# Two edits to a decoder trunk: where the feed-forward's down steps stand, and a written order for layer A's first projections

## The chip, the cores and the metric

The kernel runs on one core of one Trainium2 chip. The metric is the time of one execution on the device, in microseconds; less is better. Several engines of the core work side by side and wait for each other by semaphores: TensorE (PE) multiplies matrices and transposes, with its weight loads shown as an engine of their own (PEld); VectorE (DVE) and ScalarE (ACT) work element by element and are the ones here that read PE's results from its banks; GpSimd (POOL) works element by element on on-chip memory; SyncE (SP) issues most transfers, and POOL issues some.

## The reference, cut to what matters

A two-layer decoder trunk over 1024 tokens of width 1024, in float32. Layer A has sparse attention, layer B dilated attention over shared keys and values; each layer ends with a gated feed-forward of hidden width 2816.

```python
h = rmsnorm(x, norm_mix[layer])
proj = h @ w_in                      # layer A: queries, three kinds of keys and values, gates
k_cmp = compress(kvh(kc), pe_k, w1_k, w2_k)
...
x = x + mix
a, b = jnp.split(rmsnorm(x, norm_ffn[layer]) @ w_up, 2, axis=-1)
x = x + (jax.nn.silu(a) * b) @ w_down
```

In layer A a table of position biases (32 buckets by 16 heads) is added to all attention scores.

## The kernel before, in words

**Precision.** Every float32 operand of a large product is split in two parts, high and low: ACT copies it to the high part (lines 348 and 351, or `ph` at line 1002) and DVE subtracts that from the operand to get the low part (lines 349 and 352, `pl` at line 1003). A product is then three matmuls (`mm3`, lines 375 to 377): high by high, high by low and low by high.

**Layer A's first stage.** It runs in three rounds over row blocks of 128 tokens: blocks 0 and 1, then 2 and 3, then 4 to 7. `norm_to_hT` normalises each block (ACT squares and sums at line 382, takes the root at 384; DVE takes the reciprocal at 385 and scales at 395), PE turns it (line 400), and ACT and DVE split the result into `hH` and `hL`. After each round `proj_T` projects the tokens that are ready to the keys that will be compressed (two weight blocks of 128 columns), and ACT and DVE copy the result to `kc2` (lines 577 to 581). After the last round come the bias table's products (`bias_rows`, lines 451 to 463, with the one-hot table loaded in four pieces), then the projection of all eight row blocks to the window values and gates (`tok_proj` with `evac_v(1)`, 304 columns), then the compression, which reads `kc2`, and the remaining projections. A small table, `blockind`, is split and stored in two halves through one buffer (lines 703 to 710). In this part nothing but the framework's planner sets the order of instructions on each engine: it lists them by program order and by when it reckons their operands to be ready, and what it has placed runs in that order.

**The feed-forward.** Hidden blocks j = 0 to 21 of 128 columns are taken in pairs. Each j has seven up steps (`cols_steps`), one Strassen-like product of four k-blocks by three matmuls each, 12 matmuls; in the trace they go by the block that they multiply: m1 B11, m2 B21, m5 T1, m6 T2, m7 T3, m4 T4, m3 B22. m1, m6, m7 and m4 add up in one bank (`ux`), with an ACT copy taken out after each of the first three (`d0` at line 1218, `d1` at 1257, `c` at 1266); m2 goes to bank `uy`, is added to `d0` by DVE (line 1227), and m5 and m3 then add up in `uy`. `d0` and `d1` are built in the pair's own blocks `u[base + 0]` and `u[base + 1]`. They go through Silu (line 1415) and are multiplied by the other half (line 1417). The four blocks `u` of a pair are taken in turn from six, so that the last two of a pair are the first two of the pair before.

Each pair also has seven down steps (`down_steps`, `rows_steps`), in the order D0 to D6, that multiply its four hidden blocks with the down weights, again 12 matmuls each. D0, D3, D4 and D6 write the banks `dx`, one after another; D1, D2 and D5 write `dr`. DVE adds the results to `xr` (line 1061). D2 and D3 first form sums of the hidden blocks and of the weights on POOL (lines 1069 to 1079). D0 issues the pair's four weight loads and, in layer 0 for some pairs, two copies of bias rows.

The up steps of a pair and the down steps of the pair before are put into one list, and `staged` prepares each step before it runs the one ahead of it. The place of the down steps in that list is this:

```python
for i, f in enumerate(steps, j == 2):
    seq.append(f)
    if i % 2 and prev:
        seq.append(prev.pop(0))
```

With the up steps of a pair counted 0 to 13, a down step follows the steps 1, 3, 5, 7, 9, 11 and 13. Here too the planner then orders each engine. Layer B's projections use the same `cols_steps`; both attentions are ordered by a planner written in the kernel (`Order`), which ends by adding an edge between each instruction and the next of its engine.

Of the kernel before, what the change touches and what calls it, by code (L numbers as in the profile page):

```python
# [11 lines left out]
F32 = mybir.dt.float32  # L12
F32R = mybir.dt.float32r
# [8 lines left out]
D = 1024  # L22
# [3 lines left out]
G = 4  # L26
# [88 lines left out]
class Order:  # L115
# [88 lines left out]
    def done(self):  # L204
# [75 lines left out]
        queued = mybir.DependencyInfo(mybir.DependencyClass.NoSync, mybir.DependencyReason.DATA)  # L280
        for e, row in order.items():
            if e == "SP":
                continue
            for a, b in zip(row, row[1:]):
                self.tc.add_manual_dep(b, a.name, queued, reason="order")
# [14 lines left out]
def trunk(ctx, tc, I, out):  # L300
# [28 lines left out]
    pool(ctx, "shift", "right").tile([128, 104], F32, name="shift")  # L329
# [4 lines left out]
    nc.vector.memset(eps, 1e-6)  # L334

# [18 lines left out]
    class Weights:  # L354
# [6 lines left out]
        def load(self, src, a, n, gains=None):  # L361
            raw, wh, wl = (r.tile() for r in self.rings)
            v = lambda t: t[:, :a * n].rearrange("p (a n) -> p a n", n=n)
            self.last = nc.sync.dma_start(v(raw), src.rearrange("(a p) n -> p a n", p=128))
            if gains is not None:
                nc.gpsimd.tensor_mul(v(raw), v(raw), gains.unsqueeze(2).to_broadcast([128, a, n]))
            split(wh[:, :a * n], wl[:, :a * n], raw[:, :a * n])
            return v(wh), v(wl)
# [19 lines left out]
    def norm_to_hT(p, xget, gains, hH, hL, t0, n):  # L388

        xs = []  # L390
        for t in range(t0, t0 + n):
            xt = xget(t)
            xn = p.tile([128, D], F32, name="nxn", bufs=4)
            rs = row_scale(p, xt, xn)
            nc.vector.tensor_scalar(xn, xt, rs, None, op0=OP.mult)
            xs.append(xn)
        for k in range(KC):
            pt = bank("mm")
            for i in range(n):
                nc.tensor.transpose(pt[:, i * 128:(i + 1) * 128], xs[i][:, k * 128:(k + 1) * 128], ident)  # L400
            tk = slice(t0 * 128, (t0 + n) * 128)
            split(hH[k][:, tk], hL[k][:, tk], pt[:, :n * 128], gains[:, k:k + 1])
# [15 lines left out]
    def tok_proj(ws, n, hT, tokens, evac):  # L418

        hH, hL = hT  # L420
        for t in range(NT):
# [29 lines left out]
    def bias_rows(p):  # L451
        rb = p.tile([33, H], F32, name="rb")
        nc.vector.memset(rb, 1.0)
        nc.gpsimd.dma_start(rb[0:32], I["rel_bias"])
        R = p.tile([H, NL], F32, name="R")
        for lo in range(0, NL, 512):
            n = min(512, NL - lo)
            oh = p.tile([33, 512], F32, name="oh", bufs=2)
            nc.gpsimd.dma_start(oh[:, :n], I["onehot"][:, lo:lo + n])
            ps = bank("mm")  # L460
            nc.tensor.matmul(ps[:H, :n], rb, oh[:, :n], start=True, stop=True)
            nc.vector.tensor_copy(R[:, lo:lo + n], ps[:H, :n])
        nc.gpsimd.dma_start(sR, R)
# [103 lines left out]
    with ExitStack() as c:  # L567
        wts = Weights([(pool(c, "pw", "right"), (3, 5, 5))])
        cctx = ExitStack()
# [22 lines left out]

        with ExitStack() as c2:
# [8 lines left out]
            kc2, ws = None, []  # L602
            for t0, n in ((0, 2), (2, 2), (4, 4)):
                norm_to_hT(np_, xget, g_mix[0], *hT, t0, n)
                if t0 < 4:
                    ws.append(blocks_weights(0, len(ws)))
                if t0 == 0:
                    kc2 = blocks_tile()
                done = t0 * 128, (t0 + n) * 128
                if t0 == 2:  # L610
                    proj_T(ws[0], hT, evac_c(kc2, 0), (done,))
                    proj_T(ws[1], hT, evac_c(kc2, 1), ((0, 512),))
                else:
                    for ch in range(len(ws)):
                        proj_T(ws[ch], hT, evac_c(kc2, ch), (done,))
        cp = pool(cctx, "pc")
        st = pool(c, "pst", "right")
# [50 lines left out]
        def evac_v(i):  # L668
            def f(t, ps):
                vt = st.tile([128, G, 128], F32R, name="vt", bufs=2)  # L670
                split(vt[:, :, 0:64], vt[:, :, 64:128], ps[:, :256].rearrange("p (g d) -> p g d", d=64))
                nc.gpsimd.dma_start(vS[i, t], f32(vt))
                if i == 1:
                    nc.vector.tensor_copy(gates[:, t, :], ps[:, 256:304])
            return f

        bias_rows(cp)
        tok_proj(wide(wts, W[:, 2304:2608], 304, 3), 304, hT, natural, evac_v(1))
# [24 lines left out]
        def store_blockind():  # L703
            for a in range(2):
                cols = slice(a * 512, (a + 1) * 512)
                raw = st.tile([16, 512], F32, name="bif", bufs=1)
                nc.gpsimd.dma_start(raw, I["blockind"][:, cols])
                t = st.tile([128, 512], F32R, name="sth", bufs=2)
                nc.scalar.copy(t[:16], raw)
                nc.gpsimd.dma_start(bS[:, cols], f32(t[:16]))  # L710

# [1258 lines left out]
```

## Time and profile before

| what | value |
|---|---|
| median of three runs | 2914.61 us (2912.68 to 2917.57) |
| profiled execution, its own time | 2911.7 us |
| its span, first to last instruction | 2909.9 us |
| mean granted TensorE clock | 0.990 |
| first transpose of layer A on PE | 8.33 us |
| first matmul of the compression | 88.03 us |
| PE busy, 0 to 88 us | 70.27 us |
| PE busy, 900 to 1400 us (feed-forward of layer A) | 498.44 us, 2169 matmuls |
| PE busy, 2340 to 2840 us (feed-forward of layer B) | 498.52 us, 2167 matmuls |

The profile lists busy time by engine. A matmul's record is longer than the distance between the starts of two matmuls, because they overlap on PE; rates are therefore read from starts and counts, not from durations. A window's row gives its length, the busy time and number of instructions of PE, PEld, DVE, ACT and POOL, the granted clock as a share, the busy share of the transfer engines and GB/s. In rows of waits the numbers are the total in us, how often, and the longest. In rows of the timeline they are the start and the duration in us.

### The profile page before, as it was taken

The page shows a single profiled execution, that of the slowest core. Times are in us where ns is not written, and L with a number is a line of the kernel's source. Part 1 is how long each engine was busy: PE and PEld are TensorE (multiplying, and loading weights), DVE is VectorE, ACT ScalarE, POOL GpSimd, SP SyncE. Part 2 cuts the span into 40 slices and gives each one's busy share as a digit, 9 for nine tenths or more (in the row PEclk, how much of TensorE's full clock was granted, in tenths as well). Part 3 has the DMA queues.
Part 4 walks back from the last instruction along what each step waited for, and adds up shares of the span by engine and source line. Part 5 has one row for each costly group of instructions (what it writes and reads, how often), then busy time and mean ns, then how long its engine had stood idle before and what let it go on. Part 6 is the DMA issues. An engine that isn't in the chain of part 4 may idle for free.

```text
span 2909.9 us, 43844 instructions
## 1 busy us (share of the span) xinstructions
PE 2817.3 (97%) x14766; PEld 2376.1 (82%) x14766; DVE 2255.6 (78%) x4465; ACT 1520.9 (52%) x3314; POOL 1540.8 (53%) x1776
## 2 busy tenths in 40 slices
PE   7999999999999999999999999899999999999997
PEld 6988899998877888888787888788877788888885
DVE  5441999997488888988876777598965888888887
ACT  5431888886443333333554444689855433333334
POOL 2134877873165555555546786455522655555551
PEclk8999999999999999999999999999999999999999
DMA  5756243212122322231225555966521221111112
GB/s 161 237 156 190 67 111 89 59 26 117 30 69 66 83 62 66 62 83 52 95 80 146 161 167 160 281 194 184 142 88 37 73 61 51 55 55 58 51 44 76
DMA packets 266833, 294.46 MB, mean 101 GB/s; under 512 B 18099, under 2 KB 209475, under 8 KB 266608
## 3 DMA queue, kind: packets, MB, share of 16 engines
q1 hardware_dynamic: 246960, 231.50, 27.5%
q0 software_dynamic: 19648, 60.16, 6.9%
q8 instruction: 117, 1.92, 0.3%
q14 instruction: 108, 0.88, 0.1%
HBM read 228.49 MB, written 78.81 MB: 106 GB/s over the span
## 4 chain that ended last, share of the span: by engine, by line
PE 72%; DVE 16%; ACT 4%; issue 3%; DMA 2%; POOL 2%; SPq 1%; DVEq 0%; ACTq 0%; POOLq 0%
PE ux L375 5%; PE ux L376 5%; PE ux L377 5%; DVE pl L1003 5%; PE pt L485 5%; DVE xr L1061 4%; PE uy L375 4%; PE uy L376 4%; PE uy L377 4%; PE dx L376 4%; PE dx L377 4%; PE dx L375 3%; PE dr L375 3%; PE mm L375 3%; PE mm L376 3%
## 5 line engine op out<-in xcount | busy, mean ns | idle before, releaser
L1003 DVE TENSOR_TENSOR pl<-oT,ph 128x512 fp32r<-128x512 f32 x325 | 323.6, 1016 | 73.2 <-ACT ph L1002 64.1
L1002 ACT ACTIVATE ph<-oT 128x512 fp32r<-128x512 f32 x325 | 196.4, 626 | 221.8 <-PE ux L376 60.2
L485 PE MATMUL pt<-ident,P 128*128 128x128 f32 x1536 | 260.3, 277 | 4.8 <-DVE tl L349 2.3
L1003 DVE TENSOR_TENSOR pl<-oTb,ph 128x512 fp32r<-128x512 f32 x235 | 218.2, 954 | 50.6 <-ACT ph L1002 42.3
L1002 ACT ACTIVATE ph<-oTb 128x512 fp32r<-128x512 f32 x235 | 140.4, 625 | 177.3 <-PE ux L376 52.5
L1061 DVE TENSOR_TENSOR xr<-xr,dr 128x512 f32<-128x512 f32 x320 | 204.6, 679 | 29.2 <-PE dr L377 29.2
L1386 POOL TENSOR_TENSOR oT<-oT,gffn 128x512 f32<-128x512 f32 x92 | 106.7, 1168 | 205.5 <-DMA oT<-in_ffn_w_up_dram 168.5
L349 DVE TENSOR_TENSOR tl<-pt,th 128x512 fp32r<-128x512 f32 (+1 forms) x320 | 194.2, 625 | 20.9 <-ACT th L348 17.3
L485 PEld LDWEIGHTS pt<-ident,P 128*128 128x128 f32 x1536 | 181.5, 141 | 28.3 <-POOL P L924 4.1
L924 POOL TENSOR_SCALAR P<-P,sm,gates 128x384 f32<-128x384 f32 (+7 forms) x256 | 182.6, 723 | 38.6 <-DVE sm L922 32.6
L1061 DVE TENSOR_TENSOR xr<-xr,dx 128x512 f32<-128x512 f32 x320 | 200.1, 680 | 2.4 <-PE dx L377 1.8
L348 ACT ACTIVATE th<-pt 128x512 fp32r<-128x512 f32 (+1 forms) x320 | 168.4, 545 | 42.9 <-PE pt L485 33.0
L1386 POOL TENSOR_TENSOR oTb<-oTb,gffn 128x512 f32<-128x512 f32 x92 | 103.8, 1138 | 154.5 <-DMA oTb<-in_ffn_w_up_dram 134.7
L920 ACT ACTIVATE P<-P,m 128x384 f32<-128x384 f32 (+7 forms) x256 | 171.1, 671 | 12.4 <-DVE m L918 9.0
L1761 ACT ACTIVATE P<-P,st 128x384 f32<-128x384 f32 (+2 forms) x256 | 139.4, 548 | 6.2 <-DVE st L1756 5.2
L376 PE MATMUL dx<-pl,ph 128*128 128x512 f32 x352 | 139.3, 396 | 1.0
L377 PE MATMUL dx<-ph,pl 128*128 128x512 f32 x352 | 136.5, 391 | 0.0
L510 PE MATMUL o<-tl,V 128*128 128x256 f32 x476 | 136.3, 304 | 0.0
L509 PE MATMUL o<-th,V 128*128 128x256 f32 x476 | 135.9, 300 | 0.2 <-DVE oTb L522 0.2
L1756 DVE CUSTOM_DVE_ANT_0 P<-s,T 128x384 f32<-128x384 f32 (+2 forms) x256 | 115.7, 478 | 15.9 <-PE s L1812 5.2
L1002 ACT ACTIVATE ph<-wd 128x512 fp32r<-128x512 f32 x86 | 53.7, 629 | 115.5 <-PE ux L376 55.0
L914 DVE CUSTOM_DVE_ANT_0 P<-s,T 128x256 f32<-128x256 f32 (+3 forms) x192 | 101.8, 551 | 6.4 <-PE s L912 4.6
(951 smaller groups left out, 9530.9 us busy)
## 6 DMA issues: line engine op xcount, KB each, us to landing
qB<-xr POOLq DMA_DIRECT2D x96, 256.0 KB, 5.1
oT<-in_ffn_w_up_dram SPq DMA_DIRECT2D x92, 256.0 KB, 3.1
oTb<-in_ffn_w_up_dram SPq DMA_DIRECT2D x92, 256.0 KB, 3.0
Q<-qB SPq DMA_DIRECT2D x40, 512.0 KB, 7.8
wd<-in_ffn_w_down_dram SPq DMA_DIRECT2D x66, 256.0 KB, 2.5
oT<-in_b_w_q_dram SPq DMA_DIRECT2D x48, 256.0 KB, 4.0
K<-kBs SPq DMA_DIRECT2D x40, 256.0 KB, 9.6
wraw<-in_a_w_in_dram SPq DMA_DIRECT2D x18, 512.0 KB, 4.7
```

Source lines behind the costliest of these rows:

```text
L348: nc.scalar.activation(H_, src, AF.Copy)
L349: nc.vector.tensor_sub(L_, src, f32(H_))
L375: nc.tensor.matmul(ps, lh, rh, start=first, stop=False, skip_group_check=bool(shared))
L376: nc.tensor.matmul(ps, lh, rl, start=False, stop=False, skip_group_check=bool(shared))
L377: return nc.tensor.matmul(ps, ll, rh, start=False, stop=last, skip_group_check=bool(shared))
L485: nc.tensor.transpose(ps[:, i * 128:(i + 1) * 128], b, ident)
L920: nc.scalar.activation(P[:, e, :n], P[:, e, :n], AF.Exp, bias=mm[:, e:e + 1], scale=-1.0, accum_out=sm[:, e:e + 1])
L924: nc.gpsimd.tensor_scalar(P[:, e, :n], P[:, e, :n], sm[:, e:e + 1], gt(g, t, br, 2 * hp + e, 1), op0=OP.mult, op1=OP.mult)
L1002: nc.scalar.activation(like(h), src, AF.Copy)
L1003: (eng or nc.vector).tensor_sub(like(l), src, f32(like(h)))
L1061: nc.vector.tensor_add(xs, xs, banks[t])
L1386: nc.gpsimd.tensor_mul(v, v, gains[:, k:k + 4].unsqueeze(2).to_broadcast([128, 4, 128]))
```

## The change

In the feed-forward, the down steps follow the up steps 2, 3, 5, 8, 10, 11 and 13 of a pair, and the first product's copy `d0` of odd j from 5 on goes into the block `c` instead of the pair's own block:

```diff
             def tmp(n):
+                if n == "d0" and j > 4 and j % 2:
+                    return misc["c"]
                 if n in ("d0", "d1"):
                     return u[base + int(n[1])]
...
             for i, f in enumerate(steps, j == 2):
                 seq.append(f)
-                if i % 2 and prev:
+                if i in (2, 3, 5, 8, 10, 11, 13) and prev:
                     seq.append(prev.pop(0))
```

In layer A's first stage, normalising, turning and splitting become separate functions; the value projection of single row blocks is put between the others; the bias products and the block indicator are drawn into the stage; and the instructions of PE, ACT and DVE, up to the last turn, get the written order as an edge from each to the next (`in_turn`, cut out of `Order`). The first weight block is loaded and split in two parts, the second and third part of the value weights are loaded into row buffers, the one-hot table is loaded at once, and a square root of one column is taken at the start.

```diff
-    pool(ctx, "shift", "right").tile([128, 104], F32, name="shift")
+    shift = pool(ctx, "shift", "right").tile([128, 104], F32, name="shift")
...
+    nc.scalar.activation(shift[:, 0:1], eps, AF.Sqrt)
...
+def in_turn(tc, rows):
+    queued = mybir.DependencyInfo(mybir.DependencyClass.NoSync, mybir.DependencyReason.DATA)
+    for row in rows:
+        for a, b in zip(row, row[1:]):
+            tc.add_manual_dep(b, a.name, queued, reason="order")
...
+        def load(self, src, a, n, gains=None, parts=None, other=None):
+            raw, wh, wl = [other() if other and r is self.rings[0] else r.tile() for r in self.rings]
...
+            for c in cuts:
+                self.last = nc.sync.dma_start(v(raw)[:, c], rows[:, c])
...
+            if parts:
+                return (v(wh), v(wl)), [lambda c=c: fill(c) for c in cuts]
...
+    def turn_rows(xs, gains, hH, hL, t0, ks):
+
+        pts = [bank("mm") for _ in ks]
+        for i, xn in enumerate(xs):
+            for k, pt in zip(ks, pts):
+                nc.tensor.transpose(pt[:, i * 128:(i + 1) * 128], xn[:, k * 128:(k + 1) * 128], ident)
+        tk = slice(t0 * 128, (t0 + len(xs)) * 128)
+        return [lambda k=k, pt=pt: split(hH[k][:, tk], hL[k][:, tk], pt[:, :len(xs) * 128], gains[:, k:k + 1])
+                for k, pt in zip(ks, pts)]
...
+            start = len(nc.cur_bb.bb.instructions)
+            bias = bias_rows(np_)
+            xs = [xget(t) for t in range(2)]
+            cols = lambda ch: W[:, 1024 + 128 * ch:1152 + 128 * ch]
+            ws = [wts.load(cols(ch), KC, 128, None, 2 - ch) for ch in range(2)]
+            wv = [wts.load(W[k * 128:min(k + 3, KC) * 128, 2304:2608], min(3, KC - k), 304, None, 1,
+                           k and (lambda: np_.tile([128, D], F32, name="nx", bufs=4))) for k in (0, 3, 6)]
+            xs += [xget(t) for t in range(2, 8)]
+            fills = [f for _, fs in ws + wv for f in fs]
...
+            xn = [normed(np_, xs[t]) for t in range(2)]
+            fs = turned(xn, 0, 0, 4)
+            run(fills[:1] + fs + fills[1:2])
+            run(turned(xn, 0, 4, 8))
+            run(fills[2:3])
+            blocks(0, 2, 0)
+            run(fills[3:])
+            blocks(0, 2, 1)
+            xn = [normed(np_, xs[t]) for t in (2, 3)]
+            values(0)
+            late = []
+            values(1, late)
+            for ks in ((0, 4), (4, 8)):
+                run(turned(xn, 2, *ks) + late)
+                late = []
+            xn = [normed(np_, xs[t]) for t in (4, 5)]
+            blocks(2, 2, 0)
+            xn += [normed(np_, xs[t]) for t in (6, 7)]
+            blocks(2, 2, 1)
+            store_blockind()
+            values(2)
+            run(turned(xn, 4, 0, 4))
+            values(3)
+            bias()
+            run(turned(xn, 4, 4, 8))
...
+            in_turn(tc, [rows[e] for e in ("PE", "Activation", "DVE")])
+            blocks(4, 4, 0, 1)
+            for t in range(4, 8):
+                values(t)
```

Here `blocks(t0, n, ch)` projects n row blocks from t0 on with weight block ch to the keys to be compressed, `values(t)` projects row block t to the window values and gates, and `bias()` makes the bias table's products. SP and POOL get no written order.

More of the change, by code (lines that the diff above doesn't have):

```diff
@@ L386, in row_scale, with normed @@
         return rs
[L388 to L402, printed above, removed]
+    def normed(p, xt):
+        xn = p.tile([128, D], F32, name="nxn", bufs=4)
+        rs = row_scale(p, xt, xn)
+        nc.vector.tensor_scalar(xn, xt, rs, None, op0=OP.mult)
+        return xn
+    def turn_rows(xs, gains, hH, hL, t0, ks):
[6 more added lines that the diff above has]
+                for k, pt in zip(ks, pts)]
     def alloc_hT(p):
@@ L416, in proj_T, with tok_proj @@
             evac(ps, tk)
-    def tok_proj(ws, n, hT, tokens, evac):
+    def tok_proj(ws, n, hT, tokens, evac, ts=range(NT)):
         hH, hL = hT
-        for t in range(NT):
+        for t in ts:
             ps = bank("mm")
@@ L452, in bias_rows, with products @@
         rb = p.tile([33, H], F32, name="rb")
-        nc.vector.memset(rb, 1.0)
+        nc.gpsimd.memset(rb[32:33], 1.0)
         nc.gpsimd.dma_start(rb[0:32], I["rel_bias"])
         R = p.tile([H, NL], F32, name="R")
[L456 to L463, printed above, removed]
+        oh = p.tile([33, NL], F32, name="oh")
+        nc.gpsimd.dma_start(oh, I["onehot"])
+        def products():
+            for lo in range(0, NL, 512):
+                n = min(512, NL - lo)
+                ps = bank("mm")[:H, :n]
+                nc.tensor.matmul(ps, rb, oh[:, lo:lo + n], start=True, stop=True)
+                nc.vector.tensor_copy(R[:, lo:lo + n], ps)
+            nc.gpsimd.dma_start(sR, R)
+        return products
     def bias_skewed(t, lo, n, pitch, h, prev):
@@ L591, in blocks_weights, with evac_v, f, store_blockind @@
             return wts.load(W[:, c0:c0 + 128], KC, 128)
+        def evac_v(i):
+            def f(t, ps):
+                vt = st.tile([128, G, 128], F32R, name="vt", bufs=2)
+                split(vt[:, :, 0:64], vt[:, :, 64:128], ps[:, :256].rearrange("p (g d) -> p g d", d=64))
+                nc.gpsimd.dma_start(vS[i, t], f32(vt))
+                if i == 1:
+                    nc.vector.tensor_copy(gates[:, t, :], ps[:, 256:304])
+            return f
+        def store_blockind():
+            for a in range(2):
+                cols = slice(a * 512, (a + 1) * 512)
+                raw = st.tile([16, 512], F32, name="bif", bufs=1)
+                nc.gpsimd.dma_start(raw, I["blockind"][:, cols])
+                t = st.tile([128, 512], F32R, name="sth", bufs=2)
+                nc.scalar.copy(t[:16], raw)
+                nc.gpsimd.dma_start(bS[:, cols], f32(t[:16]))
         with ExitStack() as c2:
@@ new lines, in trunk, with run, blocks, values @@
+            ws = [w for w, _ in ws]
+            wv = [(wh[:, i], wl[:, i]) for (wh, wl), _ in wv for i in range(wh.shape[1])]
+            kc2 = blocks_tile()
+            turned = lambda xn, t0, *ks: turn_rows(xn, g_mix[0], *hT, t0, range(*ks))
+            def run(fs):
+                for f in fs:
+                    f()
+            def blocks(t0, n, *chs):
+                for ch in chs:
+                    proj_T(ws[ch], hT, evac_c(kc2, ch), ((t0 * 128, (t0 + n) * 128),))
+            def values(t, late=None):
+                ev = evac_v(1)
+                tok_proj(wv, 304, hT, natural, ev if late is None else lambda *a: late.append(lambda: ev(*a)), (t,))
@@ new lines, in trunk @@
+            xn = [normed(np_, xs[t]) for t in (4, 5)]
[8 more added lines that the diff above has]
+            run(turned(xn, 4, 4, 8))
+            rows = {}
+            for i in nc.cur_bb.bb.instructions[start:]:
+                if not type(i).__name__.startswith("Bass"):
+                    rows.setdefault(str(i.engine).split(".")[-1], []).append(i)
@@ L701, in evac_k @@
             return f
[L703 to L710, printed above, removed]
         def evac_q(ch):
```

42 lines of the change are left out of this document (6 added, 36 removed).

## The prediction

> **What bounds the kernel now.** I read the page first, then the stages as windows, then the waits of the stages that the change touches.
>
> ```profile
> span 2909.9 us, 43844 instructions
> PE 2817.3 (97%) x14766; PEld 2376.1 (82%) x14766; DVE 2255.6 (78%) x4465; ACT 1520.9 (52%) x3314; POOL 1540.8 (53%) x1776
> ```
> ```profile
> 0.00:88.00 88.00, 70.27 (x384) 59.61 (x385) 41.08 (x81) 41.81 (x81) 20.78 (x35) 0.90 0.57 162
> 88.00:290.00 202.00, 202.00 (x1092) 175.47 (x1090) 71.44 (x99) 69.67 (x105) 57.73 (x116) 1.00 0.69 197
> 900.00:1400.00 500.00, 498.44 (x2169) 405.14 (x2168) 438.64 (x597) 188.86 (x326) 280.22 (x207) 1.00 0.24 65
> 2340.00:2840.00 500.00, 498.52 (x2167) 404.87 (x2166) 434.27 (x597) 188.61 (x326) 273.01 (x205) 1.00 0.17 52
> ```
>
> PE bounds nearly everything, so only time in which PE does nothing, or works slowly, can be won. The columns are PE, PEld, DVE, ACT, POOL, then granted clock, DMA share and GB/s. From 88 to 290 us PE is busy all the time: whatever the first stage gives back there reaches the end. The two feed-forward windows look full, and DVE is busy 88% in them, so it is the next bound.
>
> **The first 88 us.** These rows give PE's waits there, then events on PE and ACT, then two stretches.
>
> ```profile
> PE mm L400 <- DVE nxn L395: 9.6, 2, 8.3
> PE mm L400 <- DVE hL L352: 6.0, 2, 3.1
> PE mm L461 <- DMA oh<-in_onehot_dram: 1.8, 1, 1.8
> ```
> ```profile
> 5.70 1.28 ACT L384 ACT_TABLE_LOAD   x1
> 6.99 0.29 ACT L384 ACTIVATE nrs<-nss,eps 128x1 f32<-128x1 f32 x1
> 12.31 1.06 ACT L382 ACTIVATE nxn<-nx 128x1024 f32<-128x1024 f32 x1 [2.42 <-DMA nx<-in_x_dram]
> 13.36 2.28 ACT L351 ACTIVATE hH<-mm,gmix 128x256 fp32r<-128x256 f32 x6
> 21.50 0.60 ACT L709 CAST sth<-bif 16x512 fp32r<-16x512 f32 x1
> 27.35 0.62 ACT L709 CAST sth<-bif 16x512 fp32r<-16x512 f32 x1
> ```
> ```profile
> 22.89 1.01 POOL L707 DMA_DIRECT2D bif<-in_blockind_dram  x1
> ```
> ```profile
> 8.33 2.91 PE L400 MATMUL mm<-ident,nxn 128*128 128x128 f32 x12 [8.33 <-DVE nxn L395]
> 15.17 0.58 PE L375 MATMUL mm<-hH,wh 128*128 128x256 f32 x1
> 37.73 4.32 PE L400 MATMUL mm<-ident,nxn 128*128 128x128 f32 x32
> 53.21 1.89 PE L461 MATMUL mm<-oh,rb 33*16 33x512 f32 x4
> 59.92 0.62 PE L375 MATMUL mm<-wh,hH 128*128 128x304 f32 x1
> 88.03 0.28 PE L375 MATMUL cmp<-bh,wh 128*128 128x256 f32 x1
> ```
> ```profile
> 24.00:32.00 8.00, 6.37 (x26) 5.57 (x27) 7.34 (x17) 6.63 (x16) 0.48 (x1) 0.57 0.63 211
> 56.00:64.00 8.00, 7.14 (x25) 4.51 (x26) 5.36 (x9) 1.97 (x3) 0.51 (x1) 0.59 0.38 93
> ```
>
> PE waits 8.3 us for the first normalised rows, then twice about 3 us for split activations. ACT shows why: the planner put the square of the third row block ahead of the splits of the first two, and that square stood 2.42 us for its load. Behind such waits PE runs slowly: 0.57 and 0.59 of the clock. The stage ends when PE starts the compression at 88.03.
>
> **The feed-forward windows.** PE's weight loads name who is late; the rows behind them are from one odd step.
>
> ```profile
> PEld ux L375 <- ACT oT L1266: 4.0, 8, 0.5
> PEld dx L376 <- DVE pl L1003: 3.9, 8, 0.5
> PEld ux L375 <- ACT ph L1002: 2.3, 6, 0.4
> PEld dx L375 <- DVE xr L1061: 1.1, 4, 0.3
> ```
> ```profile
> 1046.98 0.39 PE L375 MATMUL ux<-B11h,ph 128*128 128x512 f32 x1
> 1049.70 0.39 PE L375 MATMUL dr<-ph 128*128 128x512 f32 x1
> 1056.27 0.39 PE L377 MATMUL uy<-B21h,pl 128*128 128x512 f32 x1
> 1056.54 1.01 PE L375 MATMUL dx<-ph 128*128 128x512 f32 x2
> 1057.66 0.50 PE L375 MATMUL ux<-T2h,ph 128*128 128x512 f32 x1
> ```
> ```profile
> 1050.90 0.69 DVE L1417 TENSOR_TENSOR oT<-oT 128x512 f32<-128x512 f32 x1
> 1055.71 2.48 DVE L1061 TENSOR_TENSOR xr<-xr,dx 128x512 f32<-128x512 f32 x4
> 1058.10 0.77 DVE L1003 TENSOR_TENSOR pl<-wd,ph 128x512 fp32r<-128x512 f32 x1
> 1059.39 0.67 DVE L1227 TENSOR_TENSOR oT<-oT,uy 128x512 f32<-128x512 f32 x1
> ```
> ```profile
> 1051.30 0.58 ACT L1218 ACTIVATE oT<-ux 128x512 f32<-128x512 f32 x1
> ```
>
> A step of 12 matmuls without a wait takes 1049.70 - 1046.98 = 2.72 us, 0.2267 us a matmul. The windows need 500 / 2169 = 0.2305 and 500 / 2167 = 0.2307. So 0.0038 x 2169 + 0.0040 x 2167 = 8.3 + 8.7 = 17 us is lost to small stalls. A pair of hidden blocks has 14 up and 7 down steps, 252 matmuls, so the windows hold 4336 / 252 = 17.2 pairs: 1.0 us each. The last rows show the largest stall: down step 4 adds into the dx banks that down step 3 filled; their four additions end at 1058.19, the second operand's split only at 1058.87, and PE, which starts two dx products at 1056.54, starts the next product at 1057.66: 1.12 us for 0.45.
>
> **The change part by part: first stage.** Work of PE up to 88.03 at full clock: 64 transposes at 4.32 / 32 = 0.135 us, 8.6 us; 96 projection matmuls of 512 columns (two weight blocks, eight k, three products, two halves) at 0.2267, 21.8 us; the bias products, eight records at 1.89 / 4, 3.8 us; the values, 88.03 - 59.92 = 28.1 us. Together 62.3 us. PE had 88.03 - 8.33 = 79.7 us for it, so 17.4 us were lost behind the first transpose.
>
> *Early square root.* The new one-column activation runs before x has landed and costs nothing there; if the tables are loaded for it, the load at 5.70 goes. It stands between the first row's square and its root at 6.99, so the first transpose comes 1.28 us sooner, at 7.05 (if the load stays, nothing is won or lost). The Trainium skill (ScalarE: Activation LUTs, What ACT_TABLE_LOAD costs) gives 1283 ns for the load and about 1380 ns of drain beside it; by that 2.7 us would be won, but here the root starts 1.29 us after the load does, so the drain does not show.
>
> *Written order, loads cut and reordered, value projection drawn forward.* No instruction of weight is added: one load of 512 KB becomes two of half the size, four one-hot loads become one, two value loads go into row buffers. The loads of x from the third row block on now queue on SP behind the value weights, and the one-hot table (33 x 1917 x 4 bytes, 253 KB, at the window's 162 GB/s 1.6 us) loads beside them; the value projection of the first two row blocks covers both. What stays lost, each an estimate: the first 16 transposes and 24 products (256 columns) still run cold. The transposes go at 2.91 / 12 = 0.243 us, so 16 x (0.243 - 0.135) = 1.7 us; half clock costs the products another 24 x 0.113 = 2.7 us. The value weights are split in order on ACT and DVE behind the first evacuations: 1 us. The block indicator is new in ACT's written queue, and its buffer is single: the second copy can run only after a load that is issued after the first; before, 22.89 to 27.35, 4.5 us. Behind it on ACT wait the evacuation of the third value product and the last splits; PE has two value products to cover it (24 x 28.1 / 192 = 3.5 us each), less what is late already: 1.5 us, between 0 and 4.5. In sum 6.9 us, so the stage ends at 7.05 + 62.3 + 6.9 = 76.3: **11.8 us sooner**. Bounds: only the cold start and none of the rest gives 14.3; all waits as today and only the table load gives 1.3.
>
> The Trainium skill (TensorE: Matmul & The Clock Gate, Part 1) says that one idle window of about 3.4 us halves the clock until PE was busy as long again. The trace has the half clock after waits of 3.1 us. By the page a full wait for the block indicator costs half of 3.4 us more, 10.1 us won instead of 11.8.
>
> **Feed-forward.** The order of a pair becomes, by up step and down step: even m1 m2 m5 D0 m6 D1 m7 m4 D2 m3; odd m1 m2 D3 m5 m6 D4 m7 D5 m4 m3 D6. Only D0, D3 and D4 move, each past one up step. No instruction is added or removed.
>
> - D4 now stands two up steps behind D3, 5.4 us instead of 2.7. The additions and the split that were late by under 2 us are then covered: the dx rows, 3.9 + 1.1, go.
> - m7 no longer follows m6 directly (the ACT copy out of bank ux lies behind D4), and D5 stands whole between m7 and m4. The 4.0 us on the ACT copy at L1266 mostly go; the 2.3 us on ph I leave.
> - D0 takes along its operand splits, four down-weight loads on SP and in layer 0 two bias copies; all pass only m5, which issues no load in the steady pairs and two sums on POOL. D3 takes four sums on POOL and two splits past m2, which issues none on POOL; D4 takes two splits past m6 and its two sums. But m5 now directly follows m2, and both use bank uy: PE must wait for DVE's addition (0.67 us) unless the planner lets D0 or m6 go first. Not shown before in this place. Bounds: 0, or in each pair the addition with DVE's backlog; at L1227 it ended 1060.06 - 1056.54 = 3.5 us behind its product.
> - D3 behind m2 means that the first product's copy (d0) may no longer go into the old block, which D3's sums still read: hence the other one. That one is read until 1051.59 by the multiplication at L1417; the copy at L1218 began at 1051.30, so it slips by some 0.4 us. m2 covers it.
>
> Removed: (5.0 + most of 4.0) of 11.3 us named, about three quarters of 17, 13 us; given back at m5 I take 3 us, 0.17 a pair, near the lower end since D0 and m6 are ready. **10 us sooner**, bounds +17 and -8 (half removed, 1 us given back a pair).
>
> **Sum.** The profiled execution took 2911.7 us, 1.8 above its span and 2.9 below the median of 2914.6. 2911.7 - 11.8 - 10 = 2889.9; at the median 2892.8. I predict 2893.
>
> **The rivals.**
> 1. The planner already puts steps where operands are ready (the trace has T2 ahead of T1), so the small stalls only move: feed-forward unchanged, 2914.6 - 11.8 = 2902.8. For it: the stalls are half microseconds, as large as what the planner misjudges. Against: the spacing of D3 and D4 doubles.
> 2. The written queue on ACT makes PE wait as long as the planner did: first stage 1.3, feed-forward 10: 2903.3. Against: today's head wait for x at 12.31 goes.
> 3. Slower: m5 behind m2. If PE's queue holds m5 directly behind m2, and DVE's addition ends 3.5 us after m2, each pair waits 3.5 us and saves 0.8: 17.2 x 2.7 = 46 less 12, 2949; with 1.8 us a pair, 17 less 12, 2920. It decides from 1.5 us a pair. Against: before, D0 and T2 did stand ahead of T1.
> 4. Neither part tells: 2912 to 2915.
>
> **How the numbers follow.** Forecast 0.65, rival 1 0.17, rival 2 0.08, rival 3 0.05, rival 4 0.05. A measurement of this kernel can tell about 0.2%, 6 us. Faster takes the first three, 0.90; same rival 4, 0.05; slower 0.05. The range is 2876 (both upper bounds: 14.3 + 17 = 31, and some of the unlisted early pairs) to 2906 (rivals 1 and 2 whole).
>
> **What would show it.** The first transpose near 7, one table load fewer in the first 10 us, the first compression product near 76, the clock above 0.57 from 24 to 32, and an ACT wait of 2 to 4 us on the block indicator. In the feed-forward windows some 2190 products in 500 us instead of 2169, no dx waits on pl, and any new wait of T1 on the addition at uy. Wrong if the compression starts after 84 us, or the products per 500 us do not rise.

## The result

| | kernel before | changed kernel |
|---|---|---|
| median, us | 2915.27 | 2894.15 |
| lowest to highest | 2912.68 to 2917.57 | 2889.54 to 2897.01 |
| ratio after / before, 95% interval | | 0.9928 (0.9916 to 0.9940) |
| profiled execution, its span | 2909.9 | 2895.2 |
| first matmul of the compression | 88.03 | 77.89 |
| first score matmul of attention A | 288.69 | 281.80 |
| feed-forward of layer A, first B11 to last B22 | 632.60 | 626.18 |
| layer B's projections, first B11 to first score | 366.60 | 372.35 |
| feed-forward of layer B, first B11 to last B22 | 632.74 | 626.14 |

21.1 us were won, 0.7%; 2893 was forecast. The stage lengths in this and the later tables are differences of start times in the trace's timeline. Among the timed executions of the experiments two, at mean clocks of 0.194 and 0.779, took 13549 and 3352 us; the medians and ranges below leave them out.

The busy times of the changed kernel, from its page:

```profile
PE 2807.2 (97%) x14790; PEld 2378.2 (82%) x14790; DVE 2301.4 (79%) x4467; ACT 1520.2 (53%) x3317; POOL 1552.9 (54%) x1774
```

TensorE's products are of the same columns (24 more matmuls, because some of 512 columns became two of 256), and it is busy 10.1 us less for them: part of the gain is work at a higher clock. The windows of the changed kernel, with the columns as before (PE, PEld, DVE, ACT, POOL, granted clock, DMA share, GB/s):

```profile
0.00:78.00 78.00, 65.72 (x409) 58.22 (x410) 40.49 (x80) 39.67 (x81) 18.53 (x32) 0.98 0.66 179
78.00:282.00 204.00, 202.05 (x1081) 174.39 (x1079) 72.91 (x101) 72.16 (x107) 59.47 (x118) 1.00 0.68 197
900.00:1400.00 500.00, 499.39 (x2190) 409.93 (x2189) 460.31 (x607) 191.48 (x329) 286.47 (x208) 1.00 0.25 66
2340.00:2840.00 500.00, 499.23 (x2191) 410.28 (x2190) 460.33 (x607) 191.24 (x329) 276.24 (x204) 1.00 0.18 53
```

The first stage runs at clock 0.98 where it had 0.90 (neither figure holds the cold start: the window from 7 to 10 us reads 1.00 while the transposes are slow). The second row is new in kind: before, TensorE was busy in all 202.00 us between the compression and attention A; now it stands for 1.95 us there. The feed-forward windows hold 2190 and 2191 products where they held 2169 and 2167.

Events of the first stage, from the timeline of ACT and then of PE:

```profile
0.72 1.28 ACT L337 ACT_TABLE_LOAD   x1 [0.72 <-PEq L2017]
...
5.55 0.29 ACT L393 ACTIVATE nrs<-nss,eps 128x1 f32<-128x1 f32 x1
```
```profile
6.99 1.11 PE L409 MATMUL mm<-ident,nxn 128*128 128x128 f32 x4 [6.99 <-DVE nxn L401]
8.47 3.28 PE L409 MATMUL mm<-ident,nxn 128*128 128x128 f32 x12 [0.37 <-DVE nxn L401]
...
11.98 0.41 PE L386 MATMUL mm<-hH,wl 128*128 128x256 f32 x1
12.19 0.32 PE L384 MATMUL mm<-hH,wh 128*128 128x256 f32 x1
12.34 0.28 PE L385 MATMUL mm<-hL,wh 128*128 128x256 f32 x1
...
77.89 0.29 PE L384 MATMUL cmp<-bh,wh 128*128 128x256 f32 x1
```

The only table load of the head now lies ahead of the data, and the root at 5.55 finds its table. The first transposes are still cold (12 in 2.93 us, 0.244 us each), but the products come at 0.15 us a piece by 12.19, at 0.12 from 12.34 on: three of them are cold, not 24 (eight in a second profile of this kernel).

### The profile page after: what moved, and what is told of

Its sections match the earlier page's. It is cut to its first block, busy times and chain, and to the rows that moved or that the text cites. A ratio compares the mean times of both kernels' runs of the same rounds, so it can differ in the third digit from the quotient of the medians.

```text
span 2895.2 us, 43984 instructions
## 1 busy us (share of the span) xinstructions
PE 2807.2 (97%) x14790; PEld 2378.2 (82%) x14790; DVE 2301.4 (79%) x4467; ACT 1520.2 (53%) x3317; POOL 1552.9 (54%) x1774
## 4 chain that ended last, share of the span: by engine, by line
PE 79%; DVE 9%; ACT 3%; issue 3%; DMA 3%; POOL 2%; SPq 1%; DVEq 0%; POOLq 0%; ACTq 0%
PE ux L384 6%; PE ux L385 6%; PE ux L386 6%; PE uy L384 5%; PE uy L385 5%; PE uy L386 5%; PE pt L500 5%; PE dx L384 4%; PE dx L385 4%; PE dx L386 4%; PE dr L384 3%; PE dr L386 3%; PE dr L385 3%; PE mm L385 2%; PE o L525 2%
## 5 line engine op out<-in xcount | busy, mean ns | idle before, releaser
L1060 DVE TENSOR_TENSOR pl<-oT,ph 128x512 fp32r<-128x512 f32 x325 | 335.7, 1049 | 65.6 <-ACT ph L1059 49.1
L1060 DVE TENSOR_TENSOR pl<-oTb,ph 128x512 fp32r<-128x512 f32 x235 | 234.4, 1017 | 42.8 <-ACT ph L1059 26.7
L384 PE MATMUL mm<-hH,wh 128*128 128x512 f32 (+1 forms) x272 | 103.2, 379 | 1.2 <-ACT wh L351 1.2
```

Source lines behind the costliest of these rows:

```text
L384: nc.tensor.matmul(ps, lh, rh, start=first, stop=False, skip_group_check=bool(shared))
L1060: (eng or nc.vector).tensor_sub(like(l), src, f32(like(h)))
```

## The experiments

**Each half alone.** *First stage alone*: the changed kernel with the two feed-forward edits taken back.

```diff
-                if n == "d0" and j > 4 and j % 2:
-                    return misc["c"]
...
-                if i in (2, 3, 5, 8, 10, 11, 13) and prev:
+                if i % 2 and prev:
```

> The changed kernel with the feed-forward as before (down steps after the odd up steps, first copy in the pair's own block): the first stage's edits alone. Theory: the two parts are separate. The compression starts at 77.9 us as in the changed kernel, attention of layer A starts about 7 us sooner than before (1.9 us of the 10 are lost when attention opens its banks, and more while the compression's weights are split), the feed-forward windows hold 2168 matmuls in 500 us as before, and the time is 2915.3 - 7 = 2908. Rival: the shift of the first stage does not pass through the kernel (transfers set the start of attention), the time is within 2 us of 2915.

*Feed-forward alone*: the kernel before with the two feed-forward edits.

```diff
+                if n == "d0" and j > 4 and j % 2:
+                    return misc["c"]
...
-                if i % 2 and prev:
+                if i in (2, 3, 5, 8, 10, 11, 13) and prev:
```

> The kernel before with only the feed-forward edits (places of the down steps, first copy of odd blocks in another block). Theory: 2189 matmuls in 500 us of each feed-forward instead of 2168, 6.5 us less in each of the two feed-forwards, the first stage as before, the time 2915.3 - 13 = 2902. Rival: part of it came from the shift in time against transfers, then fewer than 2185 matmuls and less than 10 us. In both: the projections of layer B, whose instructions stand in the same order in all these kernels, took 366.6 us before and 372.4 us in the changed kernel; if that is the scatter of single executions, this run lies anywhere from 365 to 373 there, if the edit of the feed-forward costs it, near 372.

| | median (range) | ratio to before (95%) | first compression product | first score | FFN A | layer B's projections | FFN B |
|---|---|---|---|---|---|---|---|
| before (beside them) | 2913.37 (2907.74 to 2917.36) | | 88.03 | 288.69 | 632.60 | 366.60 | 632.74 |
| first stage alone | 2911.62 (2903.43 to 2914.28) | 0.9992 (0.9981 to 1.0002) | 77.85 | 280.74 | 633.77 | 371.94 | 631.55 |
| feed-forward alone | 2894.85 (2891.07 to 2902.24) | 0.9940 (0.9918 to 0.9961) | 86.36 | 287.02 | 626.19 | 368.30 | 625.35 |

(The stage columns of the first row are from the first profile of before.) The first stage does what it does in the whole change: by these profiles it is 10 us sooner at the compression and 8 us sooner at the first score. The end gains 1.8 us, which can't be told from nothing and lies between my expectation and its rival. The feed-forward alone gives 18.5 us, all but 3 of the whole; 6.4 + 7.4 = 13.8 us of it are seen in the two stages, the rest lies within the interval. My expectation for it, 2902, was too timid. Its windows and the longest of the weight loads' waits in the first window:

```profile
900.00:1400.00 500.00, 499.39 (x2191) 410.01 (x2190) 460.08 (x608) 192.47 (x331) 293.55 (x210) 1.00 0.25 65
2340.00:2840.00 500.00, 499.38 (x2192) 410.63 (x2192) 460.43 (x607) 191.46 (x330) 275.79 (x204) 1.00 0.18 53
```
```profile
PEld ux L375 <- ACT oT L1266: 4.0, 8, 0.5
PEld dx L376 <- DVE pl L1003: 0.6, 2, 0.3
```

The dx waits went from 3.9 to 0.6 us, those on `ph` and `xr` are gone, and the 4.0 us on the ACT copy have not moved by a tenth.

**Which of the three moved down steps carries it.** *D0 stays*: the changed kernel, with D0 back behind the up step 1.

```diff
-                if i in (2, 3, 5, 8, 10, 11, 13) and prev:
+                if i in (1, 3, 5, 8, 10, 11, 13) and prev:
```

> The changed kernel with down step 0 back behind the second up step; only down steps 3 and 4 stand one up step later. Theory (the gain is the double distance of down steps 3 and 4): 2187 to 2190 matmuls in 500 us, no difference from the changed kernel. Rival (moving down step 0 gives time to the additions of down step 6 in the same banks): 2175 to 2183, with waits of down step 0 on the additions into xr.

*D4 alone*: D0 and D3 at their old places, D4 moved; the first product's copy stays in the pair's own block.

```diff
-                if n == "d0" and j > 4 and j % 2:
-                    return misc["c"]
...
-                if i in (2, 3, 5, 8, 10, 11, 13) and prev:
+                if i in (1, 3, 5, 7, 10, 11, 13) and prev:
```

> The changed kernel with down steps 0 and 3 back at their old places and down step 4 one up step later, the first copy in the pair's own block as before. Down step 4 then has three up steps between it and down step 3. Theory (the distance alone decides): the waits of down step 4 on splits and additions go as in the changed kernel, 2186 to 2190 matmuls in 500 us. Rival (the up steps 2 and 5, which share a bank, and 5 and 6 now follow each other without a down step between, and wait): the waits move to the fifth block (T1), 2172 to 2182 matmuls.

With D0 at its old place the windows hold 2192 and 2190 products, the feed-forwards take 625.09 and 625.22 us and the kernel took 2890.43 us: moving D0 does nothing. D4 alone took 2919.11 us in its one execution. Its feed-forwards take 632.03 and 634.25 us, against 632.60 and 632.74 before, and its windows hold fewer products than either theory had. Its windows, the longest of its weight loads' waits from 900 to 1400, and DVE and PE in one pair:

```profile
900.00:1400.00 500.00, 495.11 (x2162) 403.80 (x2160) 453.10 (x600) 187.18 (x326) 282.29 (x207) 1.00 0.25 64
2340.00:2840.00 500.00, 491.79 (x2150) 402.13 (x2149) 448.18 (x594) 187.18 (x326) 274.18 (x205) 1.00 0.18 53
```
```profile
PEld ux L386 <- DVE pl L1060: 8.8, 12, 1.0
```
```profile
1046.71 2.47 DVE L1118 TENSOR_TENSOR xr<-xr,dx 128x512 f32<-128x512 f32 x4
1049.10 0.99 DVE L1060 TENSOR_TENSOR pl<-oT,ph 128x512 fp32r<-128x512 f32 x1
```
```profile
1049.26 0.39 PE L385 MATMUL ux<-T2l,ph 128*128 128x512 f32 x1
1050.14 0.50 PE L386 MATMUL ux<-T2h,pl 128*128 128x512 f32 x1 [0.50 <-DVE pl L1060]
```

The dx waits are gone here too, as D4 is three up steps behind D3. But D3 still stands ahead of m2, and in the trace m2 and then m6 follow it with nothing between: D3's four additions hold DVE from 1046.71 to 1049.1, and only then does it split the operand of m6 (T2), whose third product waits 0.65 us longer than its step of 0.2267. The stall is of the same kind as the one removed and is larger. In the changed kernel, where D3 has moved behind m2 as well, no weight load of `ux` waits for a split. So the gain needs D3's move beside D4's; D3's by itself was not tried.

**Where the first stage's gain goes: the opening of attention A.** The first score product waits for a split (`stl`) that it doesn't multiply. The changed kernel projects to the compressed keys in six pieces where before there were five; all take their banks in turn, so I supposed that the first score's bank is now the one that the last split still reads. *Other banks*: the order in which attention A's pools open, and with it the physical banks of its scores, is changed; the order of all instructions stays.

```diff
-        c.push(open_banks(("s",), ("pt",), ("o",), turn=True))
+        c.push(open_banks(("pt",), ("s",), ("o",), turn=True))
```

> The changed kernel with the banks of layer A's attention opened in another order (those for turning first, those for scores second); nothing else differs and the order of every engine stays the same. Theory: the first scores wait for the split of the last projection (1.4 us on PE) because the changed number of banks used before puts the first score bank on the bank of the last projection; with other banks the wait goes, the stretch from the first compression product to the first score falls from 203.9 to about 202, the time by 1.5 to 2 us to 2892. Rival: the first scores wait for the high and low parts for another reason (or the wait moves to the next bank): no difference in that stretch.

PE's longest wait from 78 to 284 us, changed kernel, then other banks:

```profile
PE s L893 <- DVE stl L355: 1.4, 1, 1.4
```
```profile
PE s L968 <- DVE m L971: 0.3, 1, 0.3
```

The wait went, and the first score comes 201.29 us after the compression's first product. It was 203.91 and 202.86 in two profiles of the changed kernel, 202.9 in most others with its first stage, and 200.66 before. The supposition holds: 1.6 of the 2.2 us usually lost there were the bank; the other 0.6, and the 1.05 more of the first profile, are open. The median was 2887.85 us (2885.98 to 2889.02; ratio 0.9912, 0.9894 to 0.9929), some 6 us below the changed kernel and more than the 2 that I expected; in its profile layer B's projections took 366.95 us instead of 372.35, which the edit doesn't touch. That is most of what it gained at the end.

**Layer B's projections.** Two kernels were run once more, unaltered: *first stage alone, again*, and *before, again*.

> The same kernel as the first stage's edits alone, a second execution under the profiler. The first stage gave 10.2 us back until the compression, but the whole kernel only about 2; 5.4 of the rest went in the projections of layer B (371.9 us against 366.6 before), whose instructions are the same in the same order. Theory (scatter: there PE stands 1 to 3 us for value blocks whose buffers wait for a store to land, and a stand over some length is followed by half clock): this execution gives another value, somewhere from 365 to 373. Rival (the shift of the first stage sets it): 371 to 373 again.

> The kernel before once more under the profiler. Theory (scatter): the projections of layer B take anywhere from 365 to 373 us, and the other stages repeat within 1 us (first stage 88 us, first to last up step of a feed-forward 632 us). Rival (set by the kernel): 366 to 367 again.

They took 2907.39 and 2910.86 us, with layer B's projections at 371.28 and 369.75. Before had 366.60 in its first profile, so 3 us of this stage are scatter.

The other stages were expected to repeat within 1 us, and the first one did not: in the second profile of before the compression starts at 86.21 us, not 88.03, and in feed-forward alone, with the same first stage, at 86.36. The eight profiles with the new first stage, its written order and one indicator buffer have 77.12 to 79.49 us, 78.4 in the mean, against 86.9 for the three with the old one. So the new first stage is worth 8.4 us at this place; the 10 us above compare a late profile of before with an early one of the changed kernel.

Most of the 1.8 us between the two profiles of before is in the clock: the window from 56 to 64 us reads 0.59 in the first profile of before and 0.79 in the second, and 0.20 x 8 = 1.6 us. The granted clock can differ between two executions behind the same stand of PE. The opening of attention A shows it for one kernel, the first stage alone, in its two profiles; in both PE has just stood 1.4 us for `stl`:

```profile
282.00:290.00 8.00, 7.91 (x39) 7.11 (x38) 5.65 (x33) 4.96 (x21) 3.50 (x12) 0.58 0.68 206
```
```profile
282.00:290.00 8.00, 7.32 (x51) 6.12 (x51) 5.92 (x37) 5.56 (x26) 4.75 (x16) 1.00 0.64 184
```

From the first score to the feed-forward the one takes 506.24 us and the other 501.83. *Changed, again* puts the question of layer B's projections to the changed kernel, with its time:

> The changed kernel, unaltered, for a second profile beside the kernel with the three further edits. Theory: the scatter lies in layer B's projections, the other stages repeat: first compression product 77 to 79 us, feed-forwards 626 us each, first score 203 to 204 us after the first compression product, layer B's projections anywhere from 364 to 373 us; time 2889 to 2897 us. Rival: layer B's projections stay at 372 within 1 us, so that their length belongs to this kernel and is not scatter.

Its median was 2896.97 us (2895.38 to 2898.23; ratio 0.9943, 0.9928 to 0.9958), first compression product 78.16, feed-forwards 625.62 and 625.26, layer B's projections 373.25. The rival fits better: the stage stays long, in two profiles of this kernel. Of the nine profiles with the new first stage and the old buffers, seven have 371.1 to 373.3 us here, *D0 stays* 365.83 and *other banks* 366.95; the three with the old first stage have 366.60, 369.75 and 368.30.

What is in those 5 us is plain. The whole stage in the profile of before, and then of the changed kernel:

```profile
1467.65:1834.25 366.60, 358.81 (x1624) 295.15 (x1623) 252.51 (x289) 173.02 (x282) 247.65 (x275) 1.00 0.52 152
```
```profile
1453.60:1825.95 372.35, 361.96 (x1624) 297.31 (x1622) 256.29 (x289) 172.29 (x282) 249.35 (x275) 0.99 0.51 149
```

For the same products TensorE is busy 3.1 us longer, at a lower clock, and stands 10.4 us instead of 7.8. In the clock of the two traces the stage has one stretch of 3.4 us at half clock before, and three in the changed kernel, 10.2 us; at half clock they cost 1.7 and 5.1 us. Without the standing and these the stage takes 366.60 - 7.8 - 1.7 = 357.1 and 372.35 - 10.4 - 5.1 = 356.8 us, and 356.0 to 357.5 in every profile taken. One such place in the changed kernel, on ACT and on PE:

```profile
1563.04 0.38 ACT L351 ACTIVATE oT<-dx 128x256 fp32r<-128x256 f32 x1 [3.71 <-DMA vBs<-oT]
```
```profile
1564.03 0.30 PE L1677 MATMUL dx<-ident,d 128*128 128x128 f32 x1 [2.29 <-DVE oT L352]
...
1566.22 0.63 PE L384 MATMUL ux<-T3h,ph 128*128 128x512 f32 x1
```

ACT can't write the next value block until the store of an older one has landed, since three buffers go round; PE stands 2.3 us behind it and from 1565.3 to 1568.7 runs at 0.43 us a product, where 0.23 is its pace. In *D0 stays* PE stands 2.4 us at 1518.9, and the 8 us behind that stand are at full clock:

```profile
1521.30:1529.30 8.00, 8.00 (x35) 6.64 (x36) 4.13 (x5) 4.20 (x7) 5.23 (x7) 1.00 0.35 133
```

*Value buffers* gives that ring four blocks more, out of rows that nothing else uses at that time:

```diff
-        wu, vts = Turns(scratch[0:10]), Turns(scratch[10:13])
+        wu, vts = Turns(scratch[0:10]), Turns(scratch[10:13] + [xr[:, r, 512 * h:512 * h + 512] for r in (2, 3) for h in (0, 1)])
```

> The changed kernel with seven instead of three buffers for the value blocks of layer B's projections (four of them in rows of the stream's tile that are free there). Theory: PE's three stands there come from stores that have not landed, which is where executions differ; the projections of layer B fall from 372 (366 before) to 357 to 361 us, no half clock remains there after the first 60 us, and the time falls by 6 to 12 us to about 2886. Rival: the stands come from DVE and ACT being busy with splits; 366 to 372 us as now, and the time within 2 us of 2894.

The waits for stores are gone from ACT's list, the stage takes 363.69 us, not as little as I expected, because PE still stands 6.5 us for other operands from ACT and DVE, and the median is 2886.52 us (2885.58 to 2889.19; ratio 0.9911, 0.9893 to 0.9929). Against the first profile of the changed kernel the stage is 8.7 us shorter: about 3.9 less standing, 5.1 less of low clock. By the medians the kernel gains 7.6 us. How much of the second part the buffers won is not certain: *D0 stays* has no low clock in this stage either, without the edit, at 8.7 us of standing. The store waits themselves are as long before as after (11.3 and 10.3 us on ACT). Why low clock follows more of the stands in kernels with the new first stage, more than 1000 us earlier, is open: layer B's instructions stand in the same order in both. The three profiles with the old first stage have one or two stretches of it, seven of the nine others three or four, and *D0 stays* and *other banks* none and one.

**Inside the first stage.** *No written order*: the changed kernel without the edges between its instructions.

```diff
-            in_turn(tc, [rows[e] for e in ("PE", "Activation", "DVE")])
```

> The changed kernel without the written order of the first stage: its instructions are issued as the program names them. Theory: the written order itself fills TensorE; without it the first compression product comes 3 us or more later than the 77.9 of the changed kernel, and the feed-forwards stay at 626 us. Rival: taking away the activation table load and the order of the program give the gain alone; first compression product within 1 us of 78. Either way at most 3 us in the end-to-end time, by what the change of the first stage alone gave.

*Two indicators*: the block indicator's copy gets a second buffer.

```diff
-                raw = st.tile([16, 512], F32, name="bif", bufs=1)
+                raw = st.tile([16, 512], F32, name="bif", bufs=2)
```

> The changed kernel with two buffers for the block indicator in place of one, so that its second conversion does not wait for the transfer behind the first. Theory: ScalarE's 3.88 us wait goes, and TensorE's stand of 2.1 us ahead of the bias products with it: first compression product 75.5 to 76.5 us. Rival: TensorE waits for the banks or for another conversion there, and the first compression product stays at 77.5 to 78.5 us.

Without the written order the first compression product comes at 82.03, where the changed kernel's first stage has 77.12 to 79.49 and the old one 86.21 to 88.03: about 5 of the 8.4 us won at this place come from the program's own order with the early root, 3.6 from the edges, each within some 1.5 us by this scatter. PE waits there, up to 82 us, 4.9 us for split activations, where it waits 0.6 in the changed kernel:

```profile
PE mm L409 <- DVE hL L355: 4.9, 2, 4.2
```

At the end this is not to be seen: 2893.57 us (2891.76 to 2896.66; ratio 0.9929, 0.9913 to 0.9946), no worse than the changed kernel. Its first score comes 201.29 us after the first compression product: without the edges PE does not wait for `stl` there, and that gives 1.6 us back at once (that another bank is taken there is not shown).

The block indicator was the larger surprise. ACT and PE of the changed kernel, then the clock of that stretch:

```profile
40.56 0.60 ACT L624 CAST sth<-bif 16x512 fp32r<-16x512 f32 x1
45.05 0.62 ACT L624 CAST sth<-bif 16x512 fp32r<-16x512 f32 x1 [3.88 <-DMA bif<-in_blockind_dram]
```
```profile
46.86 3.68 PE L474 MATMUL mm<-oh,rb 33*16 33x512 f32 x8 [2.01 <-issue]
```
```profile
46.00:54.00 8.00, 7.14 (x26) 4.04 (x27) 5.95 (x12) 3.20 (x7) 3.12 (x5) 0.79 0.31 85
```

The same with two buffers:

```profile
40.59 1.12 ACT L624 CAST sth<-bif 16x512 fp32r<-16x512 f32 x2
```
```profile
44.81 3.39 PE L474 MATMUL mm<-oh,rb 33*16 33x512 f32 x8
```
```profile
46.00:54.00 8.00, 8.00 (x40) 5.55 (x39) 5.14 (x8) 2.42 (x4) 4.18 (x6) 1.00 0.29 66
```

ACT's wait for the second transfer is gone, PE's stand of 2.0 us with it, and the clock stays full. The first compression product comes at 74.25, 3.6 us sooner than in the first profile of the changed kernel and more than I expected, because 0.21 x 8 = 1.7 us of low clock went with the 2.0 us of standing. The one time was 2891.71 us. The price of this stand is no constant: in the second profile of the changed kernel ACT waits 2.8 us and PE stands 0.9, but the clock behind it is lower, 0.42 x 8 = 3.4 us:

```profile
46.00:54.00 8.00, 8.00 (x26) 4.47 (x25) 4.85 (x11) 2.07 (x5) 2.26 (x3) 0.58 0.31 83
```

**All three together.** The changed kernel with other banks, value buffers and two indicators:

> The changed kernel with three further edits: the seven-bank rotation of the projections (so that the first scores of attention A take another bank), one more buffer for layer B's value blocks, and a second buffer for the block indicator. Theory: the three remove separate stands. First score about 201 us after the first compression product (203.9 in the changed kernel's profile), layer B's projections 363 to 366 us, first compression product near 76.5; time 2880 to 2885 us. Rival: the first two edits each gave their 6 us by the same thing, the scatter of layer B's projections, and so do not add: 2886 to 2889 us.

(The ring gets four more value blocks here too, not one as that text says, and the banks are changed as in *other banks*, by the order in which the pools open.) First compression product 74.13, first score 276.67, layer B's projections 363.89; median 2883.75 us (2880.37 to 2888.14), ratio to before 0.9899 (0.9883 to 0.9915), 13.2 us under the changed kernel beside it on the chip. The stage lengths show that the three edits remove different stands; whether their gains add in full the scatter of the medians doesn't tell. The first score came 202.54 us after the compression, not 201, without a wait for `stl`; why is open. This version is faster than both kernels.

## Why the prediction was right, and where it was not

The time was 1 us from the forecast, but the split was not the one predicted: 11.8 us from the first stage and 10 from the feed-forward were written down; alone, the two gave 1.8 and 18.5. That the sum came so close is luck.

- **Early root.** First transpose 6.99 (7.05 predicted), and the load at 5.70 is gone. Right.
- **First stage at the compression.** 77.89 and 78.16 against 76.3: 10 us won there by the profile that the prediction had, 8.4 in the mean of all profiles, not 11.8. The work was taken too long: the 28.1 us of the values were called full clock, but their first 2.6 us ran at half clock (they lie in the window from 56 to 64 us, at 0.59). At 0.14 us a product, the pace of the changed kernel, the 192 products take 26.9, and the work is 61.1 us, not 62.3. So 77.89 - 6.99 - 61.1 = 9.8 us are lost, 6.9 predicted, and the terms differ. The cold transposes cost 16 x (0.244 - 0.135) = 1.7, as written. The cold products cost 3 x 0.1 = 0.3 (0.8 in the second profile), not 2.7. The block indicator costs 3.6, not 1.5: an ACT wait of 2 to 4 us was foreseen (3.88 came), but the cover of two value products was counted too high, and the low clock behind the stand was left out of the sum. Waits that I did not list, on the first weight block's second piece and its split, come to 2.0 us by these rows of PE's waits up to 78 us:

```profile
PE mm L384 <- ACT wh L351: 1.2, 1, 1.2
PE mm L386 <- DVE wl L352: 0.8, 1, 0.8
```

  The Trainium skill (TensorE: Matmul & The Clock Gate, Part 1) has an idle window halve the clock for about 3.4 us, which by the prediction's sentence meant 10.1 us won instead of 11.8. This case's first trace agrees with the size, 1.7 us of low clock behind the stand; the second has 3.4, two such stretches. That 88.03 - 77.89 is 10.1 too is chance, since neither time repeats. The traces don't agree that the idle time must be 3.4 us: the stand was 2.0 and 0.9 us here, and 2.3 us in layer B.
- **"Whatever the first stage gives back there reaches the end."** This step failed. PE was full from 88 to 290 us before, but that said nothing of the banks at the end of it: 2 to 3 us went to the opening of attention A, of which the bank explains 1.6. Much of the rest went in layer B's projections, where standing took 2.6 us and low clock 3.4 us more than in the profile of before; that it is the new first stage that lengthens them is not shown.
- **Feed-forward, what goes.** 2190 products per 500 us were named as the sign, and 2190 and 2191 came. The dx waits went (5.0 to 1.0), the ones on `ph`, which I had left standing, went as well (2.3). The ones on the ACT copy, which were to "mostly go", stayed whole. The weight loads' waits of the changed kernel from 900 to 1400:

```profile
PEld ux L384 <- ACT oT L1323: 4.0, 8, 0.5
PEld dx L385 <- DVE pl L1060: 1.0, 3, 0.4
```

  The step that failed is that D5 "stands whole between m7 and m4". The list has it so, but had it so before the change; the trace has PE take two D5 products ahead of m7 and four between it and m4, as before, so that the copy (1058.05, 0.58 us long, on ACT) is late again. And D4, put between m6 and m7, covers the copy behind m6 (line 1257), not this one behind m7. In *D4 alone* the planner left all six D5 products of that place between m7 and m4, and no wait for this copy appears. One odd j of the changed kernel, on PE:

```profile
1043.26 0.39 PE L386 MATMUL uy<-B21h,pl 128*128 128x512 f32 x1
1043.49 1.07 PE L384 MATMUL dx<-ph 128*128 128x512 f32 x4
...
1046.21 0.39 PE L384 MATMUL uy<-T1h,ph 128*128 128x512 f32 x1
...
1057.54 0.39 PE L385 MATMUL dr<-pl,ph 128*128 128x512 f32 x1
...
1058.22 0.39 PE L386 MATMUL dr<-ph,pl 128*128 128x512 f32 x1
1058.69 0.50 PE L384 MATMUL ux<-T4h,ph 128*128 128x512 f32 x1
```

- **Feed-forward, what is given back.** I took 3 us for m5 behind m2 in bank `uy`. None came: no row of T1 waiting on the addition appears. For odd j, as in the rows above, D3 lies between m2 (B21) and m5 (T1); for even j the planner put D0 and most of m6 there, the way out that the prediction named. With that the windows lose 500 - 2190 x 0.2267 = 3.5 us each, and 17 - 7 = 10 us were won in them, the size forecast, from errors that cancel: T4's 4.0 us stayed, the 2.3 us on `ph` went, and the 3 us were not given back. The stages whole give 6.4 + 6.6 = 13.0.
- **D0, D3, D4.** The edits were costed together. The runs part them: D0's move is worth nothing, D4's alone wins nothing, and D3's with D4's is all of it (how D3's alone would do is open).
- **Rivals.** The unchanged feed-forward (2902.8) and the slower one (2920 to 2949) are out by the feed-forward alone, 2894.85. A slow ACT queue (2903.3) is out as a whole; in part it is the block indicator's 3.6 us. "Neither part tells" holds for the first stage alone at the end of the kernel, by another way than the prediction had.

## What to carry to other kernels

A gain at one place is to be followed to the next places where buffers change hands: a bank rotation that ends on another bank, or a ring that waits for stores to land, can take it back far from the edit, and a window in which the engine is full doesn't exclude that. Two consumers of a slow second engine are best spaced on both sides: moving one of them alone (D4) left the stall with the next operand in that engine's queue. Where a planner orders the work, the order written in the program tells what it may do, and the trace of the built kernel what it did.

## What was not expected of the hardware

- A stand of 2.0 us (first stage) and one of 2.3 us (layer B) were followed by a clock of 0.79 over 8 us, or 0.43 us a product for 3.4 us, and so cost about 1.7 us more than themselves. But the length of a stand doesn't tell what follows it: 0.9 us was followed by 0.58 over 8 us, 2.4 us by full clock, and 1.4 us by 0.58 in one execution and by full clock in another of the same kernel.
- Stores issued by POOL held a value block so long that ACT, with three blocks in turn, stood up to 3.7 us for one; with seven in turn it did not stand at all.
- The timed executions of one kernel differ by up to 10 us (before: 2907.74 to 2917.36), and between two profiles of before layer B's projections differ by 3 us and the first stage by 1.8 the other way.
